# Mixture-of-experts stage: packed products over columns of one k tile, paired gate and up chunks, another merge order, an earlier count

## The chip, the cores and the metric

The kernel runs on one core of a Trainium2 chip. The metric is the device time of one execution in microseconds (us). Engines are named as in the profile: PE (TensorE matmuls), PEld (its weight loads), DVE (VectorE), ACT (ScalarE), POOL (GpSimd), SP (SyncE, which here issues the large DMAs).

## The reference, cut to what matters

Two decoder layers on 256 tokens of width 1024. The first has a dense channel mixer. The second routes each token to 2 of 8 experts; this part is what the change touches:

```python
def swiglu(x, w_gate_up, w_down):
    g, up = jnp.split(x @ w_gate_up, 2, axis=-1)
    return (jax.nn.silu(g) * up) @ w_down

def moe_swiglu(x, w_router, w_gate_up, w_down):     # w_gate_up (8, 1024, 7168), w_down (8, 3584, 1024)
    logits = (x @ w_router).astype(jnp.float32)
    top_v, top_i = lax.top_k(logits, TOP_K)
    gates = jax.nn.softmax(top_v, axis=-1)
    combine = jnp.sum(jax.nn.one_hot(top_i, N_EXPERTS, dtype=jnp.float32) * gates[..., None], axis=-2)
    y = jnp.zeros_like(x)
    for e in range(N_EXPERTS):
        y = y + combine[..., e:e + 1].astype(x.dtype) * swiglu(x, w_gate_up[e], w_down[e])
    return y
```

All is float32. The expert weights alone are 8 x 44 MB = 352 MB, each byte read once.

## The kernel before, in words

Up to 614 us the kernel does layer 0, and layer 1's token mixer and routing; none of that code changes except for line numbers. Then `moe` works through the experts, ordered by how many tokens they got: place 0 has the most, place 7 the fewest. Places 0 to 3 are the **big** ones, with 128 token slots (place 0 has a second, **far**, tile of 64 slots). Places 4 and 5 have 64 slots, 6 and 7 have 32; these are the **small** ones. `gather` collects a place's tokens into columns by a product with a one-hot matrix, and after the last product the rows are sent back with the transposed one-hot (`back`), scaled by the gate and added to `acc`.

Two generators run beside each other. `big` does places 0, 1, 2, 3 in PSUM banks `mm`; `small` does 6, 7, 4, 5 in banks `aux`. `merge` interleaves their steps by two ratios, `((42, 42), (126, 49))`: 42 steps of each, then 126 big and 49 small, with the last 8 small ones (`lead`) behind everything. A big step loads 1 MB of weights, a small step 2 MB, except the 14 small steps of the last down projection (`tail`), of 1 MB and 512 columns wide. Each load is a DMA of 512 KB into a `raw` buffer, issued by SP: from `load` (L127) for big steps, from `whole` (L157) for small ones. There are 17 `raw` buffers.

- A big step splits each raw tile into a rounded part `whi` (ACT, L181) and a remainder `wlo` (DVE, L182), and PE adds three products hi*hi, hi*lo and lo*hi, each one pass of 512 columns (the far tile holds the high and low half of its tokens side by side and needs two). A raw buffer is free after its DVE instruction.
- A small step multiplies the raw float32 weights (`plain_mm`). 64 slots use half of the array's columns, 32 a quarter, so two or four products run beside each other. Before, these are **two or four different k tiles** with the same 512 weight columns, so that each strip of PSUM holds a partial sum. `copied` (L1040) brings the rows to SBUF, and `fold` (L1049) transposes all four 128-column blocks on PE and adds the partial sums (L1052, L1057). A raw buffer is free after its last product.

Up projections go by chunks of 1024 columns, first gate, then up, and of 512 at the end (`up(c, width)`). What a step leaves for PE, such as folds and transposes, is put off by `later_on` to the next `flush`. Each engine takes its instructions in the order that the scheduler wrote.

At the end comes `overflow`: every engine loads the count `omaxi` (L1294) and branches on it (L1295); the body, for experts with more tokens than slots, is not entered in these runs. Then the last LayerNorm follows, and the store.

Of the kernel before, what the change touches and what calls it, by code (L numbers as in the profile page):

```python
# [8 lines left out]
F32 = mybir.dt.float32  # L9
# [48 lines left out]
class Body:  # L58
# [397 lines left out]
    def mixer(self, l, xT):  # L456
# [72 lines left out]
        def in_turn(products):  # L529

            made = []
            for x in products:
                self.mm(*x)
                made.append(self.made.ins)
            for x, y in zip(made, made[1:]):
                self.behind(y, x, mybir.DependencyClass.NoSync)

        def fox():
            for t in range(2):
# [3 lines left out]
                for g in range(t + 1):  # L543
# [8 lines left out]
                    in_turn((p3[b][:, i], qk["fq"][rows[b], 2 * g + i, t * 128:(t + 1) * 128],  # L552
# [12 lines left out]
                    in_turn((o[rows[b], (2 * g + i) * 128:(2 * g + i + 1) * 128],  # L565
# [7 lines left out]
        def diff():  # L573
            for t in range(2):
                o = self.o_bank()
                kw = 128 * (t + 1)
                for g, n in ([(0, 4)] if t == 0 else [(0, 2), (2, 2)]):
# [6 lines left out]
                    in_turn((p3[c][:, i], qk["dq"][c * 64:c * 64 + 64, g + i, t * 128:(t + 1) * 128],  # L584
# [341 lines left out]
    def gather(self, h, place, w, far):  # L926
# [38 lines left out]
        back = self.wk.tile([128, 256], F32R, name="back", tag="back" + "sb"[big], bufs=3 if big else 2)  # L965
# [20 lines left out]
    def plain_mm(self, outs, slots, x, k0, w, loads, first, last):  # L986


        order = []
        m = 128 // slots  # L990
        for i0 in range(0, len(w), m):
            for n, out in enumerate(outs):
                for i in range(m):
                    self.mm(out[slots * i:slots * (i + 1)], x(k0 + i0 + i), w[i0 + i][:, n * 512:(n + 1) * 512],
                            first and i0 == 0, last and i0 + m == len(w))
                    order.append(self.made.ins)
        for x in loads:
            self.behind(order[0], x.ins, mybir.DependencyClass.Sync)
        for x, y in zip(order, order[1:]):
            self.behind(y, x, mybir.DependencyClass.NoSync)  # L1000
# [16 lines left out]
    def gated(self, bks, slots, out):  # L1017

        nc = self.nc
        if slots == 128:  # L1020
            for bk in bks:
                s = self.wk.tile([128, 512], F32, name="silu", tag="silu", bufs=2)
                nc.scalar.activation(s, bk, AF.Silu)
                out.append(s)
            return
        rows = self.copied(bks)

        def f():
            for r in rows:
                x = self.pk.tile([128, 256], F32, name="gcol", tag="gcol", bufs=4)[:, :4 * slots]  # L1030
                self.fold(r, x, slots)
                nc.scalar.activation(x, x, AF.Silu)
                out.append(x)
        self.later_on(f)
# [9 lines left out]
    def fold(self, r, x, slots):  # L1044
# [5 lines left out]
        x3 = x.rearrange("p (k s) -> p k s", s=slots)  # L1050
        if slots == 32:
            nc.vector.tensor_reduce(x3, tb.rearrange("p (k a s) -> p k s a", a=4, s=32), axis=AX, op=OP.add)  # L1052
            return
# [3 lines left out]
        nc.vector.tensor_add(x3, r3, t3[:, :, 0:64])  # L1057

    def hidden(self, gs, bks, slots, cells, out, plain):

        nc = self.nc
        if slots < 128:
            rows = self.copied(bks)

            def f():
                for g, r, cell in zip(gs, rows, cells):
                    u = r[:, 256:256 + 4 * slots]
                    self.fold(r, u, slots)
                    if plain:
                        x = cell[:, :4 * slots]  # L1070
                        nc.vector.tensor_mul(x, u, g)
                        out.append(x.rearrange("p (k s) -> p k s", s=slots))
                        continue
# [17 lines left out]
    def job(self, wg, wd, tiles, gates, place, acc, banks, tail):  # L1091

# [7 lines left out]
        plain = place > 3  # L1100

        def cell(slots, pool, tag, bufs):

            if plain:
                return pool.tile([128, 256], F32, name="eh", tag=tag, bufs=bufs)
# [4 lines left out]
        def up(c, width):  # L1110

            nk = (4096 if plain else 2048) // width
            gs = [[] for _ in tiles]
            for j in range(2):
                bks = [[] for _ in tiles]
                for k0 in range(0, KT, nk):
                    src = wg(k0, nk, j * FE + c, width)
                    wpc = self.whole(src) if plain else self.piece(src)
                    for n, (slots, x, _) in enumerate(tiles):
                        if k0 == 0:  # L1120
                            bks[n] = [bank() for _ in range(width // 512)]
                        if plain:
                            self.plain_mm(bks[n], slots, x()[0], k0, *wpc, k0 == 0, k0 + nk == KT)
                        else:
                            self.tile_mm(bks[n], slots, x()[0], k0, wpc, k0 == 0, k0 + nk == KT)
                    self.flush()
                    for n, (slots, _, _) in enumerate(tiles):
                        if k0 + nk < KT:
                            continue
                        if j == 0:  # L1130
                            self.gated(bks[n], slots, gs[n])
                        else:
                            self.hidden(gs[n], bks[n], slots, [cell(slots, *tiles[n][2]) for _ in bks[n]], hid[n], plain)
                    yield 1

        def down(k0, nk, c0, width):
            last = k0 + nk == FE // 128
            src = wd(k0, nk, c0, width)
            wpc = self.whole(src) if plain else self.piece(src)
            for n, (slots, _, _) in enumerate(tiles):  # L1140
# [9 lines left out]
                if plain:  # L1150
                    self.plain_mm([dn[hf, n] for hf in hfs], slots, x, k0, *wpc, k0 == 0, last)
                else:
                    self.tile_mm([dn[hf, n] for hf in hfs], slots, x, k0, wpc, k0 == 0, last)
# [26 lines left out]
        def ups():  # L1180
            for c in range(0, FE, 1024):
                yield from up(c, min(1024, FE - c))

        def downs():
            if tail:
                steps = [(4 * i, 4, 512 * hf, 512) for hf in range(2) for i in range(7)]
            else:
                nk = 4 if plain else 2
                steps = [(nk * i, nk, 0, 1024) for i in range(28 // nk)]
            for i, (k0, nk, c0, width) in enumerate(steps):  # L1190
                down(k0, nk, c0, width)
                if k0 + nk == FE // 128:
                    end(range(c0 // 512, (c0 + width) // 512))
                yield 1
        return ups(), downs()

    def moe(self, ctx, h, routing, g, b):
# [27 lines left out]
        for place in range(1, NE):  # L1225
            if place < 4:
                tiles[place] = [lazy(place, 128, self.wk, "eh", self.neh)]
            else:
                tiles[place] = [lazy(place, 64 if place < 6 else 32, pool, "near", 8)]

        def chain(places, banks, tail=None):

            for k, place in enumerate(places):
# [4 lines left out]
                up, down = self.job(*weights(eid[place]), tiles[place], lambda: gates, place, acc, banks, place == tail)  # L1238
                yield from up
                for n, z in enumerate(down):  # L1240
                    if n == 4 and k + 1 < len(places):
                        tiles[places[k + 1]][0][1]()
# [19 lines left out]
        for x in tiles[0] + tiles[6]:  # L1262
            x[1]()
        for n, z in enumerate(merge(big, small, ((42, 42), (126, 49)), 8)):
            if n == 6:
                both, overi, mxi = next(routing)
                gates += both
            if n == 12:
# [15 lines left out]
        self.overflow(h, gates, overi, mxi, weights, eid, acc, stats)  # L1284
# [6 lines left out]
    def overflow(self, h, gates, overi, mxi, weights, eid, acc, stats):  # L1291

        nc, tc = self.nc, self.tc
        n = nc.values_load(mxi[0:1, 0:1], min_val=-S, max_val=S)  # L1294
        with tc.If(n > 0):  # L1295
# [7 lines left out]
    def rest(self, h, pos, gates, w, place, base, acc):  # L1303
# [5 lines left out]
        for t in range(2):  # L1309
            nc.vector.tensor_scalar(col[:, t:t + 1], pos[t][:, place:place + 1], -float(base), None, op0=OP.add)  # L1310
            x = self.wk.tile([128, 512], F32, name="o_hot", tag="silu", bufs=2)
# [15 lines left out]
        for c in range(7):  # L1327
# [11 lines left out]
            s = self.wk.tile([128, 512], F32, name="silu", tag="silu", bufs=2)  # L1339
# [28 lines left out]
    def run(self):  # L1368
        with ExitStack() as early, ExitStack() as later:
# [78 lines left out]
```

## Time and profile before

| | us |
|---|---|
| median of 3 runs (lowest, highest) | 1533.03 (1532.88, 1535.96) |
| the profiled execution, its own time | 1533.21 |
| its span, first to last instruction | 1531.5 |
| first expert DMA is issued | 614.3 |
| last product of the experts ends | 1513.8 |
| granted TensorE clock, mean | 0.994 |

The difference of 1.7 us between time and span lies around the execution. The page gives PE as busy for 98% of the span; but ends of matmuls are modelled there, and a PE that is busy need not be what the rest waits for. So the table's stages have to be read with the bandwidth beside them.

### The profile page before, as it was taken

What the parts mean: (1) busy time and instruction counts of PE and PEld (TensorE: products, weight loads), DVE (VectorE), ACT (ScalarE), POOL (GpSimd) and SP (SyncE); (2) the same over time, 40 slices, a digit from 0 to 9 for tenths busy, and PEclk for the clock granted to TensorE, in tenths of its full rate; (3) what the DMA queues carried; (4) which work ended last, traced back from release to release, by engine and by line L of the source; (5) the groups of instructions that cost most, each with busy time, mean ns of one, the idle gap of its engine ahead of it and who ended that gap; (6) DMA issues with size and microseconds to landing.
All of it is one profiled execution on the core that took longest, in us unless ns stands there. A gap on an engine that the chain in (4) does not pass through costs nothing. (4 is left out here: it accounts for less than half of the span.)

```text
span 1531.5 us, 24214 instructions
## 1 busy us (share of the span) xinstructions
PE 1494.3 (98%) x8782; PEld 1129.4 (74%) x8782; DVE 917.5 (60%) x1302; ACT 735.6 (48%) x1049; POOL 16.8 (1%) x43
## 2 busy tenths in 40 slices
PE   8999999999999999999999999999999999999995
PEld 6989989998798997766655665666766667666662
DVE  7556675545665666444535443766666566666774
ACT  5565444444346532354434333556564556556650
POOL 3000000000000000000000000000000000000000
PEclk9999999999999999999999999999999999999998
DMA  9644546555573330999999999999999999999992
GB/s 300 195 138 140 172 159 197 189 166 179 157 238 115 127 122 1 368 409 402 408 408 403 404 401 401 409 409 402 371 405 409 383 403 409 389 396 401 397 397 100
DMA packets 187347, 454.73 MB, mean 297 GB/s; under 512 B 13050, under 2 KB 68370, under 8 KB 187220
## 3 DMA queue, kind: packets, MB, share of 16 engines
q1 hardware_dynamic: 186432, 452.05, 79.0%
q0 software_dynamic: 784, 1.05, 0.4%
q8 instruction: 71, 1.16, 0.3%
q14 instruction: 56, 0.46, 0.1%
q10 hardware_dynamic: 4, 0.01, 0.0%
HBM read 452.00 MB, written 1.05 MB: 296 GB/s over the span
## 5 line engine op out<-in xcount | busy, mean ns | idle before, releaser
L182 DVE TENSOR_TENSOR wlo<-raw,whi 128x1024 fp32r<-128x1024 f32 (+2 forms) x524 | 617.0, 1201 | 354.7 <-ACT whi L181 349.2
L181 ACT ACTIVATE whi<-raw 128x1024 fp32r<-128x1024 f32 (+2 forms) x524 | 529.6, 1041 | 269.9 <-PE mm L92 155.8
L92 PE MATMUL mm<-hTh,wlo 128*128 128x256 f32 x672 | 192.2, 286 | 0.0
L92 PE MATMUL mm<-hTh,whi 128*128 128x256 f32 x672 | 191.4, 285 | 0.0
L92 PE MATMUL mm<-hTl,whi 128*128 128x256 f32 x672 | 190.9, 284 | 0.0
L92 PE MATMUL mm<-wlo,xh 128*128 128x512 f32 x448 | 180.0, 402 | 3.1 <-DVE wlo L182 2.6
L92 PE MATMUL mm<-whi,xl 128*128 128x512 f32 x448 | 175.3, 391 | 0.0
L92 PE MATMUL mm<-whi,eh 128*128 128x512 f32 x504 | 162.9, 398 | 0.7 <-ACT whi L181 0.7
L92 PE MATMUL aux<-raw,xs 128*32 128x512 f32 (+1 forms) x896 | 156.2, 598 | 0.0
L92 PE MATMUL mm<-whi,xh 128*128 128x512 f32 x448 | 154.7, 404 | 1.2 <-ACT whi L181 1.1
L92 PEld LDWEIGHTS mm<-hTh,wlo 128*128 128x128 f32 x672 | 128.9, 192 | 2.9 <-issue 2.0
L92 PEld LDWEIGHTS mm<-hTl,whi 128*128 128x128 f32 x672 | 128.8, 192 | 0.2
L92 PEld LDWEIGHTS mm<-hTh,whi 128*128 128x128 f32 x672 | 128.8, 192 | 0.2
L92 PEld LDWEIGHTS mm<-whi,eh 128*128 128x128 f32 x504 | 92.5, 188 | 38.3 <-issue 10.0
L92 PEld LDWEIGHTS mm<-whi,xh 128*128 128x128 f32 x448 | 80.7, 188 | 46.2 <-issue 15.7
L92 PE MATMUL mm<-wlo,eh 128*128 128x512 f32 x280 | 107.7, 398 | 0.3
L92 PEld LDWEIGHTS mm<-wlo,xh 128*128 128x128 f32 x448 | 84.1, 188 | 26.6 <-DVE wlo L182 10.2
L92 PEld LDWEIGHTS aux<-raw,xs 128*32 128x32 f32 (+1 forms) x896 | 41.4, 123 | 82.0 <-issue 77.5
L1040 ACT ACTIVATE rows<-aux 128x512 f32<-128x512 f32 x56 | 33.3, 596 | 134.5 <-PE aux L92 134.5
L92 PEld LDWEIGHTS mm<-whi,xl 128*128 128x128 f32 x448 | 84.3, 188 | 16.7 <-issue 0.8
L92 PE MATMUL aux<-raw,eh 128*32 128x512 f32 (+1 forms) x448 | 78.7, 599 | 0.0
L92 PEld LDWEIGHTS mm<-wlo,eh 128*128 128x128 f32 x280 | 52.6, 188 | 12.2 <-DVE wlo L182 0.9
(325 smaller groups left out, 1940.3 us busy)
## 6 DMA issues: line engine op xcount, KB each, us to landing
raw<-in_w_expert_gate_up SPq DMA_DIRECT2D x448, 512.0 KB, 10.1
raw<-in_w_expert_down SPq DMA_DIRECT2D x224, 512.0 KB, 9.8
raw<-in_w_in SPq DMA_DIRECT2D x36, 1024.0 KB, 5.4
raw<-in_w_ffn_gate_up SPq DMA_DIRECT2D x22, 1024.0 KB, 5.1
raw<-in_w_ffn_down SPq DMA_DIRECT2D x10, 1024.0 KB, 4.9
raw<-in_w_out SPq DMA_DIRECT2D x8, 1024.0 KB, 5.0
raw<-in_w_in SPq DMA_DIRECT2D x8, 520.0 KB, 4.9
raw<-in_w_branch_fox SPq DMA_DIRECT2D x4, 1024.0 KB, 5.0
```

The costliest lines, as they stand in the source:

```text
L92: self.made = self.nc.tensor.matmul(out, lhsT, rhs, start=start, stop=stop)
L181: return (self.nc.scalar.activation(hi, src, AF.Copy), self.nc.vector.tensor_sub(lo, src, hi.bitcast(F32)))
L182: self.nc.vector.tensor_sub(lo, src, hi.bitcast(F32)))
L1040: self.nc.scalar.activation(r, bk, AF.Copy)
```

## The change

Four things, all in the experts' stage.

1. **Columns instead of k tiles.** `plain_mm` now gives the array's halves or quarters other columns of one k tile. `cuts` says into how many column ranges a step's weights are cut: in the up projection as many as there are strips (32 slots: four ranges of 256; 64 slots: two of 512), so that each strip holds finished sums of its columns and nothing is folded. The down projection always has two cuts; in the `tail` they are 256 wide. A new `plain_job` does the small places: SiLU is read from PSUM (`gsilu`), the product with up is read from PSUM as well (`rows`, L1192), and only the hidden values are transposed (L1199). The way back is by plain float32 products of 64 rows, in pairs.
2. **Gate and up by neighbouring chunks.** Gate and up columns stand beside each other, 7 chunks of 512 each; chunks are now loaded in pairs, always 1024 columns, in the order 0, 6, 2, 8, 4, 10, 12, where chunk 6 is the last of gate and 7 the first of up. SiLU tiles live longer, so `silu` has 4 buffers, not 2.
3. **Merge** goes by `((42, 37), (126, 54))`, and place 6 is gathered ahead of place 0.
4. **The count** is loaded at the 60th merged step on all engines.

Buffers: `raw` goes from 17 to 13 of 512 KB.

```diff
-    def plain_mm(self, outs, slots, x, k0, w, loads, first, last):
-        order = []
-        m = 128 // slots
-        for i0 in range(0, len(w), m):
-            for n, out in enumerate(outs):
-                for i in range(m):
-                    self.mm(out[slots * i:slots * (i + 1)], x(k0 + i0 + i), w[i0 + i][:, n * 512:(n + 1) * 512],
-                            first and i0 == 0, last and i0 + m == len(w))
+    def plain_mm(self, out, slots, cuts, x, k0, w, loads, first, last, swap=False):
+        parts = 128 // slots
+        kk = parts // cuts
+        n = w[0].shape[1] // cuts
+        products = []
+        for i0 in range(0, len(w), kk):
+            for j in range(cuts):
+                for i in range(i0, i0 + kk):
+                    q = (j * kk + i - i0 + (parts // 2 if swap else 0)) % parts
+                    products.append((out[slots * q:slots * (q + 1), :n], x(k0 + i), w[i][:, j * n:(j + 1) * n],
+                                     first and i0 == 0, last and i0 + kk == len(w)))
+        self.in_turn(products, loads)
...
+    def plain_job(self, wg, wd, tile, gates, place, acc, banks, tail):
...
+        def hidden(b, chunks):
+            r = self.row_tile("rows")[:, :n]
+            for i, h in chunks:
+                nc.vector.tensor_mul(r[half[h]], b[half[h], :n], gate[i][half[h]])
...
+            def f():
+                tb = self.tp_bank()
+                for j in range(n // 128):
+                    cs = slice(j * 128, j * 128 + 128)
+                    nc.tensor.transpose(tb[:, cs][:, rows], r[rows, cs], self.ident[rows, rows])
...
+        def up(c):
+            b = bank()
+            for k0 in (0, 4):
+                self.plain_mm(b, slots, parts, get()[0], k0, *self.whole(wg(k0, 4, 512 * c, 1024)), k0 == 0, k0 == 4, c >= 6)
+                self.flush()
...
+        def down(k0, c0, width):
+            if k0 == 0:
+                dn[c0] = bank()
+            self.plain_mm(dn[c0], slots, 2, lambda kt: hid[kt], k0, *self.whole(wd(k0, 4, c0, width)), k0 == 0, k0 == 24)
...
+        def ups():
+            for c in (0, 6, 2, 8, 4, 10, 12):
+                yield from up(c)
...
-        for x in tiles[0] + tiles[6]:
+        for x in tiles[6] + tiles[0]:
             x[1]()
-        for n, z in enumerate(merge(big, small, ((42, 42), (126, 49)), 8)):
+        for n, z in enumerate(merge(big, small, ((42, 37), (126, 54)), 8)):
...
+            if n == 60:
+                early, (most,) = nc.values_load_multi_w_load_instructions(mxi[0:1, 0:1], min_val=-S, max_val=S)
...
-                self.weights_in(ctx, "experts_w", 17, PW // 2, 5, PW // 2)
+                self.weights_in(ctx, "experts_w", 13, PW // 2, 5, PW // 2)
```

How the order of instructions moves is seen at three places. First PE, early in the experts' stage, beside place 0's up projection (`xh`, `xl`, and `xp` for the far tile) and place 6's (`raw,xs`). Before:

```order
L92 MATMUL aux<-raw,xs 32x512 x8
L1049 MATMUL tp<-ident,rows 128x128 x4
L92 MATMUL mm<-whi,xh 128x512 x2
L92 MATMUL mm<-whi,xp 128x512 x2
L1049 MATMUL tp<-ident,rows 128x128 x4
L92 MATMUL mm<-wlo,xh 128x512
```

And now, in the same place (L1051 is the far tile's fold, which stays):

```order
L92 MATMUL aux<-raw,xs 32x256 x16
L1051 MATMUL tp<-ident,rows 128x128 x4
L92 MATMUL mm<-whi,xh 128x512 x2
L92 MATMUL mm<-whi,xp 128x512 x2
L1199 MATMUL tp<-ident,rows 128x128 x2
L92 MATMUL mm<-wlo,xh 128x512
```

A small step has 16 products of 256 columns instead of 8 of 512, and two transposes of hidden values stand where eight of a fold stood. Over the stage, transposes from `rows` go from 280 to 104.

Second SP's queue, where place 6's last up chunk was loaded (ISA sets an address up). Before:

```order
L127 DMA raw<-in_w_expert_gate_up 128x1024
L157 ISA
L157 DMA raw<-in_w_expert_gate_up 128x2x512
L157 ISA
L157 DMA raw<-in_w_expert_gate_up 128x2x512
```

And now:

```order
L127 DMA raw<-in_w_expert_gate_up 128x1024
L157 ISA
L157 DMA raw<-in_w_expert_gate_up 128x1024
L157 ISA
L157 DMA raw<-in_w_expert_gate_up 128x1024
```

Each gate and up load now has rows of 1024 columns (4 KB); the two 512-wide chunks of each place, 32 MB over the eight, had rows of 2 KB. The last down projection's 14 MB and 256 KB x 4 of LayerNorm constants keep 2 KB.

Third DVE at the end of the experts. Before:

```order
L182 TENSOR_TENSOR y<-aux,y 128x512
L1162 SCALAR_TENSOR_TENSOR acc_7068<-tp,gate_6842,acc_7068 128x512
L1162 SCALAR_TENSOR_TENSOR acc_7070<-tp,gate_6846,acc_7070 128x512
L250 BN_STATS ln_st<-acc_7068 128x6
L250 BN_STATS ln_st<-acc_7070 128x6
L1294 TENSOR_LOAD omaxi
L1295 COMPARE_AND_BRANCH
```

And now:

```order
L1238 SCALAR_TENSOR_TENSOR acc_7066<-tp,gate_6846,acc_7066 128x256
L1238 SCALAR_TENSOR_TENSOR acc_7068<-tp,gate_6850,acc_7068 128x256
L1238 SCALAR_TENSOR_TENSOR acc_7066<-mm,gate_6846,acc_7066 128x256
L1238 SCALAR_TENSOR_TENSOR acc_7068<-mm,gate_6850,acc_7068 128x256
L250 BN_STATS ln_st<-acc_7066 128x6
L250 BN_STATS ln_st<-acc_7068 128x6
L1380 COMPARE_AND_BRANCH
```

The remainder `y` and the load of the count are gone from DVE's end, and the two sums are four of half the width; the branch stays. On PE the load of the count still stands right ahead of its branch.

## Rows read from the trace of the kernel before

**Rows 1.** The page: GB/s in 40 slices of the span; DMA issues.

```profile
GB/s 300 195 138 140 172 159 197 189 166 179 157 238 115 127 122 1 368 409 402 408 408 403 404 401 401 409 409 402 371 405 409 383 403 409 389 396 401 397 397 100
...
raw<-in_w_expert_gate_up SPq DMA_DIRECT2D x448, 512.0 KB, 10.1
raw<-in_w_expert_down SPq DMA_DIRECT2D x224, 512.0 KB, 9.8
```

**Rows 2.** Busy time by stretch; the columns are named in the first row.

```profile
core 0: us, PE busy (x) PEld busy (x) DVE busy (x) ACT busy (x) POOL busy (x), PEclk, DMA share, GB/s
960.00:1040.00 80.00, 79.22 (x362) 51.92 (x361) 56.11 (x62) 46.70 (x63) 0.00 (x0) 1.00 1.03 409
1090.00:1110.00 20.00, 20.00 (x106) 15.11 (x105) 12.73 (x13) 10.04 (x14) 0.00 (x0) 1.00 0.91 338
1190.00:1210.00 20.00, 20.00 (x92) 12.19 (x90) 11.87 (x11) 12.48 (x15) 0.00 (x0) 1.00 0.95 361
1300.00:1360.00 60.00, 60.00 (x270) 38.79 (x271) 41.30 (x43) 35.13 (x46) 0.00 (x0) 1.00 1.01 389
1480.00:1490.00 10.00, 10.00 (x44) 6.94 (x43) 7.35 (x6) 6.08 (x7) 0.00 (x0) 1.00 1.05 387
1500.00:1501.00 1.00, 1.00 (x7) 0.19 (x4) 0.63 (x1) 0.00 (x0) 0.00 (x0) 1.00 0.43 164
1501.00:1513.40 12.40, 12.40 (x56) 4.48 (x56) 4.01 (x6) 0.00 (x0) 0.00 (x0) 1.00 0.01 5
```

**Rows 3.** Waits of SP's DMA queue, 614.3 to 957 us: total, times, longest.

```profile
SPq L157 <- DMA raw<-in_w_expert_gate_up: 74.2, 102, 1.9
```

**Rows 4.** The same waits, 957 to 1500 us.

```profile
SPq L127 <- PE aux L92: 109.3, 69, 6.6
...
SPq L127 <- DVE wlo L182: 34.7, 42, 2.6
```

**Rows 5.** PE's groups by shape, 614.3 to 1514 us (count, busy us, mean ns).

```profile
L92 PE MATMUL aux<-raw,xs 128*64 128x512 f32 x448 | 102.3, 598 | 0.0
L92 PE MATMUL aux<-raw,xs 128*32 128x512 f32 x448 | 53.9, 598 | 0.0
...
L1049 PE MATMUL tp<-ident,rows 128*128 128x128 f32 x280 | 41.6, 276 | 1.5 <-ACT rows L1040 1.5
```

**Rows 6.** Timeline of one 32-slot step, 708 to 711 us (start, duration).

```profile
708.76 1.92 PE L92 MATMUL aux<-raw,xs 128*32 128x512 f32 x16
709.22 0.13 PEld L92 LDWEIGHTS aux<-raw,xs 128*32 128x32 f32 x4 [0.30 <-issue]
...
710.62 0.74 PE L92 MATMUL mm<-whi,xh 128*128 128x512 f32 x2
```

**Rows 7.** Timeline of layer 0's attention at 103 us, products on two halves of the array.

```profile
103.06 1.09 PE L92 MATMUL o<-pT,fv 128*64 128x128 f32 x16
```

**Rows 8.** Timeline of the end, 1495 to 1521 us.

```profile
1497.88 1.19 PE L92 MATMUL tp<-y,back 128*128 128x512 f32 x4
...
1504.99 8.80 PE L92 MATMUL aux<-raw,eh 128*64 128x512 f32 x40
...
1513.84 0.60 ACT L181 ACTIVATE y<-aux 128x512 fp32r<-128x512 f32 x1 [15.25 <-PE aux L92]
...
1515.75 1.41 DVE L1162 SCALAR_TENSOR_TENSOR acc<-tp,gate,acc 128x512 f32<-128x512 f32 x2 [0.59 <-PE tp L92]
1517.08 1.27 DVE L250 BATCH_NORM_STATS2 ln_st<-acc 128x6 f32<-128x512 f32 x2
1520.93 0.28 DVE L256 BATCH_NORM_AGGREGATE ln_mv<-ln_st 128x2 f32<-128x12 f32 x2 [2.58 <-DVEq L1295]
```

**Rows 9.** Line L1294 on DVE's and PE's queues, and L1295 (durations min/median/max in ns, first and last start).

```profile
L1294 DVEq TENSOR_LOAD <-omaxi x1: 545/545/545, 1517.2 to 1517.2; - x1
...
L1295 PEldq COMPARE_BRANCH  x1: 3875/3875/3875, 1515.8 to 1515.8; - x1
L1295 DVEq COMPARE_BRANCH  x1: 72/72/72, 1517.8 to 1517.8; - x1
```

More of the change, by code (lines that the diff above doesn't have):

```diff
@@ L984, in tile_mm, with in_turn @@
                         self.mm(out, act, part[:, n * 512:(n + 1) * 512], a and j == 0, z and j == len(steps) - 1)
[L986 to L999 removed]
+    def plain_mm(self, out, slots, cuts, x, k0, w, loads, first, last, swap=False):
[10 more added lines that the diff above has]
+        self.in_turn(products, loads)
+    def in_turn(self, products, after=()):
+        made = []
+        for x in products:
+            self.mm(*x)
+            made.append(self.made.ins)
+        for x in after:
+            self.behind(made[0], x.ins, mybir.DependencyClass.Sync)
+        for x, y in zip(made, made[1:]):
             self.behind(y, x, mybir.DependencyClass.NoSync)
@@ L1029, in f @@
             for r in rows:
[L1030 to L1031 removed]
+                x = self.pk.tile([128, 256], F32, name="gcol", tag="gcol", bufs=5)
+                self.fold(r, x)
                 nc.scalar.activation(x, x, AF.Silu)
@@ L1042, in copied, with fold @@
         return out
-    def fold(self, r, x, slots):
+    def fold(self, r, x):
         nc = self.nc
@@ L1056, in fold, with hidden @@
         nc.scalar.activation(r3, t3[:, :, 64:128], AF.Copy)
-        nc.vector.tensor_add(x3, r3, t3[:, :, 0:64])
-    def hidden(self, gs, bks, slots, cells, out, plain):
+        nc.vector.tensor_add(x.rearrange("p (k s) -> p k s", s=64), r3, t3[:, :, 0:64])
+    def hidden(self, gs, bks, slots, cells, out):
         nc = self.nc
@@ L1066, in f @@
                 for g, r, cell in zip(gs, rows, cells):
[L1067 to L1073, printed above, removed]
+                    u = r[:, 256:512]
+                    self.fold(r, u)
                     nc.vector.tensor_mul(u, u, g)
@@ L1108, in cell @@
             return pool.tile([128, 512], F32R, name="eh", tag=tag, bufs=bufs)
[L1110 to L1123, printed above, removed]
-                        else:
[L1125 to L1134, printed above, removed]
+        gs = [[[] for _ in range(7)] for _ in tiles]
+        def up(c):
+            nk = 2
+            bks = [[] for _ in tiles]
+            for k0 in range(0, KT, nk):
+                src = wg(k0, nk, 512 * c, 1024)
+                wpc = self.piece(src)
+                for n, (slots, x, _) in enumerate(tiles):
+                    if k0 == 0:
+                        bks[n] = [bank() for _ in range(2)]
+                    self.tile_mm(bks[n], slots, x()[0], k0, wpc, k0 == 0, k0 + nk == KT)
+                self.flush()
+                for n, (slots, _, _) in enumerate(tiles):
+                    for i in range(c, c + 2) if k0 + nk == KT else ():
+                        bk = [bks[n][i - c]]
+                        if i < 7:
+                            self.gated(bk, slots, gs[n][i])
+                        else:
+                            self.hidden(gs[n][i - 7], bk, slots, [cell(slots, *tiles[n][2])], hid[n])
+                yield 1
         def down(k0, nk, c0, width):
@@ L1138, in down @@
             src = wd(k0, nk, c0, width)
-            wpc = self.whole(src) if plain else self.piece(src)
+            wpc = self.piece(src)
             for n, (slots, _, _) in enumerate(tiles):
@@ L1149, in down @@
                         dn[hf, n] = bank()
[L1150 to L1153, printed above, removed]
+                self.tile_mm([dn[hf, n] for hf in hfs], slots, x, k0, wpc, k0 == 0, last)
             self.flush()
@@ L1180, in ups @@
         def ups():
-            for c in range(0, FE, 1024):
-                yield from up(c, min(1024, FE - c))
+            for c in (0, 6, 2, 8, 4, 10, 12):
+                yield from up(c)
         def downs():
[L1185 to L1193, printed above, removed]
-                yield 1
+            for k0 in range(0, 28, 2):
+                down(k0, 2, 0, 1024)
+                if k0 == 26:
+                    end(range(2))
+                yield 1
@@ L1228, in moe @@
             else:
-                tiles[place] = [lazy(place, 64 if place < 6 else 32, pool, "near", 8)]
+                tiles[place] = [lazy(place, 64 if place < 6 else 32, pool, "near", 5)]
         def chain(places, banks, tail=None):
@@ L1241, in chain @@
                     if n == 4 and k + 1 < len(places):
-                        tiles[places[k + 1]][0][1]()
+                        for x in tiles[places[k + 1]]:
+                            x[1]()
                     yield z
@@ L1267, in moe @@
                 gates += both
+            if n == 60:
+                early, (most,) = nc.values_load_multi_w_load_instructions(mxi[0:1, 0:1], min_val=-S, max_val=S)
+                order = ctx.enter_context(ExitStack())
+                for x in early:
+                    if x.ins.engine in (mybir.EngineType.DVE, mybir.EngineType.Activation):
+                        order.enter_context(tc.issue_after(x.ins))
+            if n == 62:
+                order.close()
             if n == 12:
@@ L1283, in moe @@
         stats(1)
-        self.overflow(h, gates, overi, mxi, weights, eid, acc, stats)
+        self.overflow(h, gates, overi, most, weights, eid, acc, stats)
         for t in range(2):
```

104 lines of the change are left out of this document (78 added, 26 removed).

## The prediction

> **What bounds the kernel now.** I read the page's bandwidth row first: from the 17th slice on, about 614 us, it stands near 400 GB/s to the end [rows 1]. The experts' stage moves 672 loads of 512 KB, 352 MB, and 1 MB of constants; no edit changes these bytes. So the first question is what rate the DMA could hold, the second why it holds less, the third what comes after the last byte.
>
> The best long stretch holds 409 GB/s [rows 2]. At 1480 to 1490 us, where only the last down projection's 512-wide loads run, it is 387 though the DMA engines are just as busy (share 1.05): rows of 2 KB cost 5.5% [rows 2]. At 1090, 1190 and 1300 us the rate falls to 338, 361 and 389, and there PE is busy for the whole of the stretch [rows 2]. The waits of SP say why: up to 957 us SP mostly waits for an earlier DMA, so the DMA itself sets the pace [rows 3]; after that it waits 109 us for PE to finish small products and 35 us for DVE's splits, that is, for `raw` buffers to come free [rows 4]. PE lags behind the data by nearly all 17 buffers.
>
> The end shows the lag directly. The weights are in at about 1500.5 us (the DMA is 0.43 busy in the microsecond from 1500, then 0.01) [rows 2], but PE works on until 1504.99 + 8.80 = 1513.8 us without a gap [rows 8]. These 13.3 us are backlog. So two bounds lie on each other: DMA with some 2% lost, and PE, which is nearly full and comes 13 us late.
>
> **The change part by part.**
>
> *Wider rows.* 32 MB of gate and up loads go from 2 KB rows to 4 KB rows. 33.6 MB take 86.7 us at 387 GB/s and 82.0 us at 409: **-4.7 us** of DMA time. Nothing hides it, since the DMA is never idle in the stage.
>
> *Fewer transposes.* The fold group is 280 instructions with 41.6 us of PE, 0.149 us each [rows 5]. 176 of them go: **-26 us** of PE work in the 899 us from the first load to the last product. The copies and reduces of the folds leave ACT and DVE, which are not what PE waits for at the end; I count nothing for them.
>
> *Products on other columns.* A 32-slot up step is 32 records of 256 columns instead of 16 of 512. One step now takes 708.76 to 710.62, 1.86 us [rows 6], four records in parallel, so about 0.43 us for each four. I cost the new step at the same 1.86 us. From below: twice as many products cannot take less, the columns being the same. From above: no gain from halving columns gives 3.44 us for the products. The nearest row is layer 0's attention: sixteen records of 128 columns on two halves of the array span 1.09 us, last drain included [rows 7]. Eight pairs in at most that is 0.136 us a pair for a quarter of the columns that now take 0.43 us; so the time follows the columns even at a quarter of the width. 64-slot steps keep 512 columns but for the last projection.
>
> The Trainium skill, "TensorE: Matmul & The Clock Gate", section "Part 3: Packing small matmuls — row/col tiling", says that a weight load runs beside products in flight only if it goes to other rows of the array. All strips here use all 128 rows, so by the page each group of four would wait for its weight loads. The trace disagrees: the second set of loads ends long before the products that it stands beside (0.13 us of loads, then 0.30 us idle, in each 0.43 us) [rows 6].
>
> *Merge.* Five 2 MB steps of 32 slots, 9.3 us of PE, go from beside place 0 to beside places 1 to 3. They bring 10 MB for which the DMA needs 25.6 us at 409 GB/s, so in the stretch where PE is late the work per byte falls; beside place 0 it rises, in a stretch where SP waited for the DMA. No separate gain: it lets the relief by the transposes reach both stretches.
>
> *13 buffers.* The DMA needs some loads in flight: with 10.1 us from issue to landing and 1.28 us for each at 409 GB/s, eight are queued at once on the median [rows 1]. Fewer do as well: the dips show what too few cost, 389 GB/s over 60 us [rows 2]. With 13, PE can be at most about ten loads, 13 us, late before the DMA starves. I take no cost, because PE will be less late; the bound is below.
>
> *Starved stretches.* Against 409 the three dips cost 20 x (1 - 338/409) = 3.5, 20 x (1 - 361/409) = 2.3 and 60 x (1 - 389/409) = 2.9 us, together 8.7 [rows 2]. With 26 us of PE work gone PE needs 873 us for what the DMA brings in no less than 866 (339 MB at 409 GB/s, 14.7 at 387). It stops being late for long: **-8.7 us**. Bound: 0.
>
> *The backlog.* The last 8 small steps take PE 8.80/5 = 1.76 us each [rows 8] and the DMA 2.7 us at 387 GB/s, so PE gains 7.5 us on the data, less three returns of 1.19 us [rows 8]: 4 us. If PE is 8 us late when they start, about what 13 buffers and a DMA that sets the pace leave, it ends 4 us after the last byte instead of 13.3: **-9.3 us**. Bounds: one last step and its wait, 2.2 us, and 13.3.
>
> *The end.* After PE, ACT copies 0.60 us and DVE makes a remainder before the last products; then two sums of 0.70, two statistics, the count and the branch [rows 8]. The remainder goes (0.7 us, of which the return products in plain float32 may take half back: the trace has two records for each of them, as for the `raw` products), and DVE's load of the count, 0.55 us [rows 9]. The branch's wait of 2.58 us stays [rows 8]: its target is the same, and it follows each engine's branch, not the load. PE still loads the count late, and its branch lasts to 1519.7, ahead of DVE [rows 9]. **-1.0 us**; bounds 0 and -1.3.
>
> Sum: 4.7 + 8.7 + 9.3 + 1.0 = 23.7 us from the profiled execution's 1533.2: 1509.5, say **1510 us**. That execution is 0.2 us above the median of the runs shown, so the same number stands for both.
>
> **The rivals.**
>
> *The lag stays.* The late splits may lie in the written order of ACT and PE, not in load. For it: a PE that never pauses over 60 us [rows 2] looks the same whether it has too much work or starts its work late. Against: after 957 the buffers are what SP waits for. Then the 9.3 us do not come: 1519; with half of the starved time as well, 1524.
>
> *13 buffers starve the DMA.* If more than about ten buffers are held on average, the rate is that of the dips throughout. 353 MB at 389 GB/s instead of 409 cost 44 us, against 23.7 won: 1554. Half of the stage in that state gives 1532, which is the point from which it decides. For it: SP waited for buffers even with 17 [rows 4]. Against: those waits follow PE's load, which falls.
>
> *Quarter products do not follow their columns.* If four of 256 columns take the 0.43 us of four of 512, 28 up steps take 1.72 us more, 48 us in a stretch without room: 1558. If only the weight loads come into the open, 8 groups x 0.13 us x 28 steps are 29 us of PE [rows 6], which eats the 26 us of transposes: 1531, no change. That is the time by the page's rule named above. [rows 7] speak against both.
>
> *All of it comes.* The DMA at its floor (614.3 + 866 + 2.5 us to the first landing = 1482.8, 17.7 less than now), 2.2 us of lag and 1.3 at the end are 30.1 us: 1503.
>
> **How the numbers follow.** The forecast as summed, 1503 to 1518, has 0.60. The lag that stays, 1518 to 1528, 0.20. All of it and more, below 1503, 0.06. Starving buffers 0.09, of which 0.07 slower. Quarter products 0.05: 0.03 slower, 0.02 no change (the page's rule among these, 0.02). 0.2%, 3 us, is about what a measurement of this kernel tells from no change. Faster: 0.60 + 0.20 + 0.06 = 0.86; same: 0.02 + 0.02 = 0.04; slower: 0.10. The range is 1503 to 1528: it leaves out 0.06 below and 0.14 above. It holds both cases that share the sign; the slower ones lie outside.
>
> **What would show it.** Right: 408 GB/s or more in the stretches that hold gate and up loads, without dips below 390; SP's waits for `PE aux` far under 109 us; the last load in at 1485 to 1489; PE's last product 2 to 7 us behind it; four 256-column products in about 0.22 us; DVE's gap ahead of the last LayerNorm still about 2.6 us. Wrong: a rate below 400 with SP waiting for buffers (the 13), or a 32-slot step over 2.5 us (the quarters), or 10 us and more from the last byte to PE's end (the order).

## The result and the profile after

The changed kernel takes 1524.22 us (median of 6 runs, 1523.02 to 1528.02), the kernel before 1533.81 on the same chip: a ratio of 0.9939, 95% interval 0.9925 to 0.9954. It is faster by 9.4 us by the ratio (9.6 between the medians), inside the range and far from the 23.7 us of the sum. The profiled execution took 1526.24 us, 2.0 above the median, and has a span of 1524.4 us (before 1531.5); that is why spans further down differ by 7.1 us only.

The windows of the changed kernel come first; they answer to [rows 2].

```profile
core 0: us, PE busy (x) PEld busy (x) DVE busy (x) ACT busy (x) POOL busy (x), PEclk, DMA share, GB/s
618.00:628.00 10.00, 9.79 (x46) 9.50 (x46) 3.98 (x10) 4.40 (x7) 0.00 (x0) 0.50 1.02 408
...
640.00:660.00 20.00, 20.00 (x139) 13.35 (x141) 6.57 (x6) 8.88 (x12) 0.00 (x0) 1.00 0.96 350
770.00:790.00 20.00, 19.24 (x121) 13.85 (x120) 7.90 (x8) 10.01 (x16) 0.00 (x0) 1.00 0.95 353
1250.00:1310.00 60.00, 60.00 (x278) 38.67 (x275) 37.89 (x39) 29.91 (x35) 0.00 (x0) 1.00 0.99 380
960.00:1040.00 80.00, 74.65 (x347) 47.10 (x346) 49.68 (x47) 43.13 (x48) 0.00 (x0) 1.00 1.03 409
1090.00:1110.00 20.00, 20.00 (x90) 14.38 (x91) 12.13 (x11) 8.80 (x9) 0.00 (x0) 1.00 1.03 410
...
1300.00:1360.00 60.00, 59.30 (x261) 37.13 (x260) 35.80 (x36) 29.30 (x34) 0.00 (x0) 1.00 1.02 404
...
1500.00:1503.20 3.20, 3.20 (x32) 2.15 (x30) 0.99 (x2) 0.00 (x0) 0.00 (x0) 1.00 0.72 267
1503.20:1505.20 2.00, 2.00 (x22) 1.29 (x19) 0.00 (x0) 0.00 (x0) 0.00 (x0) 1.00 0.06 20
1505.20:1507.70 2.50, 2.35 (x20) 1.26 (x16) 0.00 (x0) 0.00 (x0) 0.00 (x0) 1.00 0.00 0
```

The reader sees three things. The dips of before are gone (1090: 410 GB/s, 1300: 404), but new ones stand at 640, 770 and 1250 us. From 618 to 628 us TensorE had half of its clock, 1.2 GHz. And the DMA ends in two steps: most of it by about 1503, then 2 us at 20 GB/s and a share of 0.06, which is one of 16 engines. Looked at as closely, the kernel before does the same, which the long last window of [rows 2] had hidden:

```profile
1500.00:1501.00 1.00, 1.00 (x7) 0.19 (x4) 0.63 (x1) 0.00 (x0) 0.00 (x0) 1.00 0.43 164
1501.00:1504.00 3.00, 3.00 (x13) 1.16 (x14) 1.41 (x2) 0.00 (x0) 0.00 (x0) 1.00 0.06 19
1504.00:1506.00 2.00, 2.00 (x10) 0.98 (x12) 1.37 (x3) 0.00 (x0) 0.00 (x0) 1.00 0.00 0
```

So the last byte of before landed at 1503.9 us, not 1500.5, and TensorE ended 9.9 us behind it, not 13.3.

The timeline of TensorE at the start of the stage, in the changed kernel, shows place 6's gather (32 slots) and then place 0's (128 slots), both slow, and the first products with weights at 629.26 (place 6) and 630.68 (place 0):

```profile
616.91 5.81 PE L92 MATMUL tp<-hot,h 128*128 128x32 f32 x30 [0.22 <-DVE hot L925]
...
623.20 6.14 PE L92 MATMUL tp<-hot,h 128*128 128x128 f32 x32 [0.21 <-ACT xs L946]
629.26 1.48 PE L92 MATMUL aux<-raw,xs 128*32 128x256 f32 x18
630.68 0.50 PE L92 MATMUL mm<-whi,xh 128*128 128x512 f32 x1
```

In the kernel before, place 0's products with weights were at work ten microseconds earlier:

```profile
620.30 0.71 PE L92 MATMUL mm<-whi,xh 128*128 128x512 f32 x2
```

PE's groups by shape over the stage (to [rows 5]): the transposes from `rows` have 8.4 + 6.0 + 1.6 = 16.0 us instead of 41.6, and quarters of 256 columns 55.6 us instead of 53.9.

```profile
L92 PE MATMUL aux<-raw,xs 128*32 128x256 f32 x896 | 55.6, 382 | 0.0
...
L1051 PE MATMUL tp<-ident,rows 128*128 128x128 f32 x56 | 8.4, 280 | 1.5 <-ACT rows L1042 1.5
L1199 PE MATMUL tp<-ident,rows 128*128 128x128 f32 x36 | 6.0, 276 | 0.0
L1199 PE MATMUL tp<-ident,rows 64*128 64x64 f32 x12 | 1.6, 239 | 0.0
```

One 32-slot step in the timeline (to [rows 6], there 1.92 us for the same 2 MB), the weight loads beside it:

```profile
700.96 1.45 PEld L92 LDWEIGHTS aux<-raw,xs 128*32 128x32 f32 x32 [0.35 <-issue]
700.97 1.93 PE L92 MATMUL aux<-raw,xs 128*32 128x256 f32 x32
```

The end (to [rows 8]): `y` is copied at 1507.72, DVE's gap is 2.12 us.

```profile
1498.47 9.21 PE L92 MATMUL aux<-raw,eh 128*64 128x256 f32 x80
...
1507.72 0.38 ACT L1235 ACTIVATE y<-aux 128x256 f32<-128x256 f32 x1 [15.83 <-PE aux L92]
...
1513.86 0.28 DVE L256 BATCH_NORM_AGGREGATE ln_mv<-ln_st 128x2 f32<-128x12 f32 x2 [2.12 <-DVEq L1380]
```

The account, in us; the last column is the first experiment, explained below:

| | forecast | before | changed | place 0 gathered first |
|---|---|---|---|---|
| first load issued | | 614.3 | 614.05 | 614.5 |
| last byte, after the first load | -13.4 | 889.6 | 891.1 (+1.5) | 882.6 (-7.0) |
| TensorE's last product behind it | -9.3 | 9.9 | 2.6 (-7.3) | 2.6 (-7.3) |
| from there to the span's end | -1.0 | 17.7 | 16.7 (-1.0) | 16.8 (-0.9) |
| span | -23.7 | 1531.5 | 1524.4 (-7.1) | 1516.4 (-15.1) |

Each column is one profiled execution, so a difference of 2 us between columns says little by itself.

### The profile page after: what moved, and what is told of

Same layout as the page of the kernel before. It is cut to its first block, busy times and chain, and to the rows that moved or that the text cites. A ratio compares the mean times of both kernels' runs of the same rounds, so it can differ in the third digit from the quotient of the medians.

```text
span 1524.4 us, 24838 instructions
## 1 busy us (share of the span) xinstructions
PE 1482.7 (97%) x9174; PEld 1138.1 (75%) x9174; DVE 897.4 (59%) x1242; ACT 715.7 (47%) x966; POOL 16.9 (1%) x43
## 5 line engine op out<-in xcount | busy, mean ns | idle before, releaser
L92 PE MATMUL aux<-raw,xs 128*32 128x256 f32 (+1 forms) x1344 | 157.9, 454 | 2.1 <-issue 1.6
L92 PE MATMUL mm<-whi,xh 128*128 128x512 f32 x448 | 150.5, 404 | 0.9 <-ACT whi L181 0.9
L92 PEld LDWEIGHTS aux<-raw,xs 128*32 128x32 f32 (+1 forms) x1344 | 56.4, 118 | 83.7 <-issue 61.1
L92 PE MATMUL aux<-raw,eh 128*32 128x512 f32 (+2 forms) x560 | 79.1, 512 | 2.1 <-DMA raw<-in_w_expert_down 1.8
L92 PEld LDWEIGHTS aux<-raw,eh 128*64 128x64 f32 (+1 forms) x560 | 28.8, 125 | 38.8 <-issue 30.1
```

What stands on the lines that cost most here:

```text
L92: self.made = self.nc.tensor.matmul(out, lhsT, rhs, start=start, stop=stop)
```

## The experiments

Each ratio is to the kernel before on the same chip. "Last byte" counts from the first load, read from the DMA packets of the profiled execution.

| run | ratio, 95% interval | last byte | PE behind it |
|---|---|---|---|
| changed kernel | 0.9939 (0.9925 to 0.9954) | 891.1 | 2.6 |
| e1 place 0 gathered first | 0.9893 (0.9878 to 0.9909) | 882.6 | 2.6 |
| e2 14 buffers | 0.9920 (0.9906 to 0.9933) | 885.3 | 2.6 |
| e3 11 buffers | 0.9995 (0.9986 to 1.0004) | 899.9 | 2.6 |
| e4 before, 13 buffers | 1.0001 (0.9992 to 1.0010) | 894.4 | 5.9 |
| e5 e1 + old merge | 0.9915 (0.9901 to 0.9928) | 882.4 | 3.4 |
| e6 e1 + 14 buffers | 0.9906 (0.9893 to 0.9920) | 884.2 | 2.6 |
| e7 e1 + 15 buffers, 4 split parts | 0.9902 (0.9887 to 0.9917) | 884.0 | 2.6 |
| e8 e1 + 192 transposes | 0.9985 (0.9976 to 0.9994) | 894.5 | 7.0 |
| e9 before, place 6 first | 1.0024 (1.0015 to 1.0034) | 894.9 | 9.6 |
| e10 e1, 12.7 us of PE left out | 0.9899 (0.9884 to 0.9915) | 884.6 | 2.6 |
| e11 e1, 25.4 us of PE left out | 0.9887 (0.9871 to 0.9902) | 883.6 | 2.6 |
| e12 e7 + merge between | 0.9906 (0.9892 to 0.9920) | 882.0 | 5.0 |
| e13 e11 + 1344 instructions | 0.9883 (0.9868 to 0.9898) | 882.2 | 2.6 |
| e14 e11 + 336 longer instructions | 0.9906 (0.9891 to 0.9921) | 885.6 | 2.6 |
| e15 e1, loads of 1 MB | 1.0049 (1.0036 to 1.0063) | 899.0 | 9.0 |
| e16 e1, 152 us of PE left out | 0.9896 (0.9880 to 0.9913) | 885.0 | 2.6 |
| e17 e11 + 15 buffers, 4 split parts | 0.9887 (0.9870 to 0.9903) | 881.6 | 2.6 |

**First theories.** "Too few buffers": 13 starve the DMA. "Late start": the gather order and the clock behind it cost 9 us that TensorE cannot make up. "Merge order": the new ratios load the wrong stretch.

```diff
-        for x in tiles[6] + tiles[0]:
+        for x in tiles[0] + tiles[6]:
```

> The changed kernel (1524.2) with place 0 gathered ahead of place 6 again, all else as changed. Theory 'late start': TensorE has work without a pause from its first expert product to its last, so the 9 to 10 us by which that first product came late (630.7 us, before 620.3, with half of the granted clock for 10.2 us in between) reach the end: 1514 to 1517, the granted clock 1.00 at 616 to 630 us. Theory 'too few buffers': the start costs only the dips at 640 to 700 us (370, 331, 379 and 389 GB/s, together 4 us), and the later dips stay: 1520 to 1523. Theory 'merge order': 1522 to 1524.

Measured: 0.9893, 7.0 us less than the changed kernel's ratio gives (0.0046 x 1534). TensorE's timeline has the gather back in 4.17 us and products with weights at 620.52, and its windows the clock at 1.00 and 409 GB/s where the changed kernel had 350:

```profile
616.59 4.17 PE L92 MATMUL tp<-hot,h 128*128 128x128 f32 x32 [0.91 <-DVE hot L928]
620.52 0.71 PE L92 MATMUL mm<-whi,xh 128*128 128x512 f32 x2
```

```profile
618.00:628.00 10.00, 10.00 (x79) 9.28 (x79) 5.51 (x13) 5.19 (x8) 0.00 (x0) 1.00 1.02 409
...
640.00:660.00 20.00, 20.00 (x163) 14.15 (x156) 5.80 (x7) 8.81 (x16) 0.00 (x0) 1.00 1.02 409
...
1250.00:1310.00 60.00, 60.00 (x279) 38.01 (x278) 35.86 (x34) 30.60 (x34) 0.00 (x0) 1.00 0.99 382
...
1494.00:1497.00 3.00, 3.00 (x30) 2.01 (x28) 0.00 (x0) 0.00 (x0) 0.00 (x0) 1.00 0.17 62
1497.00:1500.00 3.00, 2.39 (x22) 1.26 (x16) 0.00 (x0) 0.33 (x1) 0.00 (x0) 1.00 0.00 0
```

0.9893 x 1533.8 is 1517.4, at the edge of what "late start" gave. The later dips stay.

Buffers: the second argument of `weights_in` is the edit.

```diff
-                self.weights_in(ctx, "experts_w", 13, PW // 2, 5, PW // 2)
+                self.weights_in(ctx, "experts_w", 14, PW // 2, 5, PW // 2)
```

> The changed kernel with 14 raw buffers instead of 13 (the room is taken from the row tiles, 5 instead of 6). Theory 'too few buffers': one more load of 1.28 us in hand in each of some seven spells in which the DMA starves, so 3 to 8 us less: 1516 to 1521. Theory 'late start': TensorE's work sets the end, and a load more in hand changes nothing: 1523 to 1525.

> The changed kernel with 11 raw buffers instead of 13. Theory 'too few buffers': the DMA runs empty in every stretch, 10 to 25 us more: 1534 to 1550. Theory 'late start': with TensorE the bound two loads less in hand cost at most 2.6 us in two or three places: 1524 to 1530.

> The kernel before with 13 raw buffers instead of 17, all else as before. It prices the four buffers where TensorE is late for most of the stage. Theory 'too few buffers': 8 us more or above, 1541 to 1555, with rates like those of the dips (338 to 389 GB/s) over long stretches. Theory 'late start': TensorE is the bound already, so the buffers cost little: 1533 to 1538.

Measured: 14 take away some 3 us (the intervals of e2 and the changed kernel overlap), 11 add 8.6 us. In the kernel before (e4) 13 cost nothing, though they are short: the last byte comes 4.8 us later, and SP waited 125.5 us for PE at L157 alone after 957 us, but TensorE's backlog set the end anyway.

```profile
SPq L157 <- PE aux L92: 125.5, 39, 7.5
```

> The kernel before with one edit: place 6 gathered ahead of place 0. Theory 'late start': the first expert product comes 8 to 11 us later here too, TensorE has no slack to make it up, and 17 buffers don't help: 1.004 to 1.007 of the time before. Theory 'too few buffers' (the late start costs only where 13 buffers run empty): 1.000 to 1.002.

Measured: 1.0024, 3.7 us, between the two. The first product with split weights came at 629.96 us, the clock was 0.66 from 618 to 628. The late start costs without the rest of the change, but in the kernel before, with 17 buffers and a backlog that is there anyway, over half of the 10 us doesn't show; which of the two hides it was not tried.

**With place 0 first, what holds the rest?**

> Place 0 gathered first (the first experiment: 0.989 of the time before), and also the merge ratios of before, (42, 42) and (126, 49). Theory 'merge order': the new ratios took five light 2 MB steps away from the first stretch and made the second stretch too heavy in small steps; with the old ones the dips at 1190 to 1330 us (360 to 394 GB/s) shrink and 3 to 6 us go: 0.985 to 0.987. Theory 'TensorE still late': the second stretch loses five steps that are light for TensorE per byte, so its dips grow, while the first stretch has more: 0.990 to 0.995. Theory 'too few buffers': no change, 0.988 to 0.990.

> Place 0 gathered first and 14 raw buffers (row tiles 5 instead of 6). Theory 'too few buffers': the dips that are left (770 to 790, 830 to 850, 1250 to 1290 us) lose some 1 us each, 0.985 to 0.987. Theory 'TensorE still late': TensorE works without a pause from one of these dips to the next, and a load more in hand is used up once and not won again: 0.988 to 0.990.

> Place 0 gathered first, 15 raw buffers, the room taken from the split weights (4 of whi and wlo instead of 5). Theory 'too few buffers': 2 to 6 us less, 0.985 to 0.988. Theory 'TensorE still late': 0.988 to 0.992, with TensorE waiting a little more for splits.

> Place 0 gathered first, 15 raw buffers (4 of whi and wlo), merge ratios (42, 40) and (126, 51), between the old and the new ones: a try for the best version. TensorE was idle for some 12 us of the stage with either ratio, at other places. Theory 'TensorE still late': the work is the same, so 0.987 to 0.990. Theory 'merge order': 0.983 to 0.987.

Measured: none differs from e1 beyond the intervals, 0.9902 to 0.9915. With place 0 first, "merge order" falls, and so does "too few buffers" from 13 up, but for effects under some 3 us, which these intervals would not show. "TensorE still late" fitted all four, so it was put to the test from both sides: transposes added (`list(range(n // 128)) * 5` in `hidden`), then products left out (the third product of `tile_mm`):

```diff
-                        steps = [(h, wh), (h, wl), (x[1](k0 + i, 0), wh)]
+                        steps = [(h, wh), (h, wl), (x[1](k0 + i, 0), wh)][:2 if k0 + i >= skip else 3]
```

> Place 0 gathered first, and each transpose of the small places' hidden values made five times into the same place: 192 more transposes on TensorE, about what the fold's 176 were. It prices the work that the change took away. Theory 'TensorE still late': TensorE's work reaches the end nearly in full, 192 x 0.11 to 0.149 us = 21 to 29 us more: 1.003 to 1.008. Theory 'too few buffers': the DMA sets the end, and half or less of it shows: 0.992 to 0.997.

> Place 0 gathered first, and in the up projections of places 0 to 3 the product of the low part of the tokens with the last of the eight k tiles is left out: 56 products of 512 columns, 0.227 us each, 12.7 us of TensorE less, which with what the change gave makes up the 26 us that were forecast. Theory 'TensorE still late': 7 to 12 us less, 0.981 to 0.985. Theory 'the DMA sets the end' (dips have another cause than TensorE): 0.988 to 0.990.

> As the one before, with the last two k tiles left out: 112 products, 25.4 us of TensorE less. Theory 'TensorE still late': now the DMA has its 409 GB/s nearly throughout, the last byte lands at 1483 to 1488 us, and the time falls by less than twice the step before: 0.975 to 0.980. Theory 'the DMA sets the end': 0.987 to 0.990.

Measured: more work costs, some 14 us (0.9985 against 0.9893) for 192 transposes that keep TensorE busy for 18.7 us, and TensorE ends 7.0 us behind the last byte. Less work gains nothing: 0.9899 and 0.9887. "TensorE still late" falls. e1 stands where more work of TensorE can be felt and less can not: something else ends there.

**What ends there.** In all runs of the changed kernel that gather place 0 first, but for e8 and e15, the last byte lands 881.6 to 885.6 us after the first load, and at the end the rate is that of one engine for some microseconds (of two in e13, below). By the packets' times 8 KB loads of the queue that the profile calls "instruction" lie in that engine's chain: in e17, below, one of 0.33 us at 1493.81, while it moves data alone. So the next runs changed the number of instructions:

```diff
+                    for j in range(4):
+                        self.nc.vector.tensor_copy(scr[0:1, j:j + 1], lo[0:1, j:j + 1].bitcast(F32))
```

> The kernel of the run with two k tiles left out (0.9887), and behind each of the 336 splits four copies of a single element on VectorE: 1344 more instructions with nearly no data. Theory 'instruction loads on one DMA engine': 1344 x 64 bytes are some 10 more loads of 8 KB on the late engine, 0.32 us each and 0.43 us of slow packets behind it, 7 to 8 us later for the last byte: 0.992 to 0.995. Theory 'the DMA engine is late for another reason': the copies take idle time of VectorE, 0.988 to 0.990.

> The same, with one copy of 256 elements on 128 partitions behind each split in place of the four: as much or more time of VectorE, a quarter of the instructions. Theory 'instruction loads on one DMA engine': 2 to 3 more loads of 8 KB, 1.5 to 2 us: 0.989 to 0.991. If the four copies cost by VectorE's time, this one costs as much as they: 0.992 to 0.995.

> Place 0 gathered first; loads of 1 MB into 7 raw buffers (row tiles 5 instead of 6) in place of 512 KB into 13: SP has half of its instructions, some 1340 fewer, and the DMA half of the loads. Theory 'instruction loads on one DMA engine': 10 fewer loads of 8 KB, the last byte 7 us earlier, if the coarser buffers don't starve the DMA: 0.984 to 0.987; with starving 0.988 to 0.995, but then the last byte of a DMA that was never short would still come sooner. Theory 'another reason': 0.989 or more.

Measured: the queue that loads them has 48 packets in the stage of e13 (the row below, 614 to 1500 us) and 37 in that of e11, and e13 is no slower (0.9883); e14, at 0.9906, is not clearly slower than e11 either. So 11 more of these loads don't cost 7 to 8 us. But that doesn't clear them, for the added ones went elsewhere: at the end of e13 two engines move data alone, 54 GB/s at a share of 0.15 (second row), where e17 has one (below). The added instructions of VectorE made a second engine about as late as the first, and the last byte did not move (882.2 against 883.6).

```profile
q14 instruction: 48, 0.39, 0.1%
...
1492.00:1496.60 4.60, 3.54 (x32) 2.19 (x28) 0.00 (x0) 0.00 (x0) 0.00 (x0) 1.00 0.15 54
```

e15 has 23 such loads, against 37 in e1, and no late engine at its end, as "instruction loads" would have it. It is still no test: 7 large buffers made SP wait 243.6 us for PE at L127, and it lost 24 us to e1.

Last, TensorE was taken out of the question: e16 leaves out 152 us of its work, e17 gives e11 two buffers more.

> Place 0 gathered first, and in places 0 to 3 every product of the low part of the tokens or hidden values with the weights' high part is left out (672 products of 0.227 us, 152 us of TensorE less; the loads are the same). Theory 'TensorE in bursts': TensorE is late only around changes of place and chunk, with so little work never; the dips go, and the last byte lands 868 to 874 us after the first load: 0.979 to 0.983 of the time before. Theory 'the DMA itself': the last byte still lands 880 to 885 us after the first load: 0.987 to 0.990.

> The kernel of the run with two k tiles left out (0.9887, last byte 883.6 us after the first load), with 15 raw buffers, the room taken from the split weights (4 instead of 5). Theory 'TensorE in bursts': two loads more in hand take up half of what the dips cost, 2 to 4 us: 0.986 to 0.988. Theory 'the DMA itself': 0.988 to 0.990.

Measured: no gain, 0.9896 and 0.9887. e17's windows show that the dips are gone, 406 GB/s at 1250 to 1310 us where e1 had 382, and that it brings nothing: 383 GB/s up to 1488, then from 1490 on for over 5 us one engine's share, 0.07.

```profile
640.00:660.00 20.00, 20.00 (x161) 13.63 (x159) 5.70 (x7) 7.98 (x14) 0.00 (x0) 1.00 1.03 409
...
1250.00:1310.00 60.00, 60.00 (x285) 39.47 (x284) 36.91 (x35) 32.27 (x37) 0.00 (x0) 1.00 1.02 406
1486.00:1488.00 2.00, 2.00 (x20) 1.18 (x18) 1.88 (x5) 0.00 (x0) 0.00 (x0) 1.00 1.04 383
1490.00:1494.00 4.00, 2.53 (x23) 1.67 (x23) 0.00 (x0) 0.00 (x0) 0.00 (x0) 1.00 0.07 26
1494.00:1496.30 2.30, 1.49 (x14) 0.86 (x10) 0.00 (x0) 0.00 (x0) 0.00 (x0) 1.00 0.06 19
1496.30:1498.00 1.70, 1.12 (x11) 0.94 (x13) 0.00 (x0) 0.00 (x0) 0.00 (x0) 1.00 0.00 0
```

Its SP waits after 957 us are nearly all for earlier DMAs:

```profile
SPq L127 <- DMA raw<-in_w_expert_gate_up: 116.6, 157, 1.5
SPq L157 <- DMA raw<-in_w_expert_gate_up: 80.4, 108, 1.5
SPq L127 <- DMA raw<-in_w_expert_down: 56.8, 75, 1.5
SPq L157 <- DMA raw<-in_w_expert_down: 45.0, 62, 1.5
SPq L127 <- PE mm L92: 6.5, 24, 0.4
```

"The DMA itself" stands.

The trace of e17 also says where the late engine loses its time. It keeps, for each load, the 16 landing times of the 16 engines' parts; their last against their eighth is how late the late engine is. From 930 to 1495 us there are 24 instruction loads of 8 KB. At 16 of them, most some 41 us apart, the last landing falls back by 0.58 to 0.74 us each; at the other 8 it doesn't, and between them it doesn't either. From 930 to 1470 us the landings lose 8.4 us against 409 GB/s, and the 13 steps in between add up to 8.7 (e16: 8.1, and 12 steps of 8.2). That the others must wait shows in SP's queue: of the 402 loads issued from 960 to 1484 us, 396 were issued within 0.2 us (median 0.12) after the last landing of the load eight before. So the late engine, one that also brings in a series of instruction loads, sets the pace of the stage from there on. This is read from traces; no run took those loads away from it.

## Why the prediction was wrong

**What was right.** The quarter products follow their columns (1.93 us a step) and the weight loads stay hidden. By the page's rule in "TensorE: Matmul & The Clock Gate", Part 3, of the Trainium skill the step would have grown by an estimated 8 x 0.13 us [rows 6]; it grew by 0.01. The transposes fell by 25.6 us (said: 26). 4 KB rows run at 404 to 410 GB/s outside the dips. The end gained the 1.0 us forecast, though in part by another way: DVE's wait ahead of the last LayerNorm, which was to stay at 2.58 us, fell to 2.12.

**The backlog: right mechanism, start mis-sized.** PE is now 2.6 us behind the last byte, one last step of 1.95 us and 0.6 us before it, near the lower bound of 2.2. But it had been 9.9 us late, not 13.3, so the gain was 7.3, not 9.3 us: the last window of [rows 2] was 12.4 us long, and its 5 GB/s were 3 us of one engine. The lag left is below the 4 us of the sum, and the lag of before was below its 13.3; the two errors partly cancel.

**The step that failed: "wider rows" and "starved stretches", the 13.4 us of DMA time.** Both were counted against 409 GB/s, with a floor of 866 us for the bytes and the last byte at 1482.8 at best, 868.5 us after the first load. No kernel came under 881.6, 13 us above that floor, not even with 152 us of TensorE's work gone, or without dips. So of the 889.6 us of before no run won more than 8.0, whatever the dips and rows cost; removing dips does not shorten a DMA whose last engine is late. What the floor left out is the instruction loads on that engine: the 16 steps counted in e17 are 10.7 of the 13 us. The rival "all of it comes" rested on the same floor.

**What was never costed: place 6 gathered first.** The sum called the merge free and passed over the gather. It made the first product with split weights 10 us late, half the clock included, against 13 buffers that hold 13 x 1.28 = 16.6 us. The buffers filled, the DMA ran short (350 GB/s at 640 to 660), and the last byte came 8.5 us later than in e1 (891.1 against 882.6). That is the sign of being wrong that the prediction named for the 13 buffers, a rate below 400 with SP waiting for buffers. SP's largest wait in the changed kernel from 614.05 to 957 us (total, times, longest):

```profile
SPq L157 <- PE aux L92: 75.6, 63, 6.1
```

So "13 buffers" at no cost failed here too: not by TensorE's load, as the rival had it, but by its start. How much 17 would have hidden in the changed kernel was not measured; one more (e2) took away some 3 us, and e3 shows that 11 would have cost another 8.6 us.

With that order undone the sum is 7.0 + 7.3 + 0.9 = 15.2 us, and e1 is the best full version found: 0.9893 against 0.9939. That the changed kernel's 1524 us is also what the prediction gave for "the lag stays; with half of the starved time as well" is chance: the lag went, to 2.6 us.

**What stays open.** Whether the stage gets shorter when the late engine's instruction loads are fewer or lie on several engines: the traces point to them, e13 added loads to another engine, and no run took any away alone. Why the lag builds up only from about 860 us in e17, though such loads come all through the stage, is open too. The Trainium skill, "DMA: Bandwidth & Descriptors", section "Latency and other measured facts", lists two engines (7 and 15) that are usually slower in traces, and guesses at rings of software DMAs. An engine that ends late agrees, a slower one doesn't: alone it moves 26 GB/s, which is a full sixteenth of 409. And the guess does not fit a stage in which the loads are issued by SP and no software queue moves a packet. Which engine it is, the trace doesn't tell. Which of the dips left in e1 belong to which change of place was not tried either.

## What to carry to other kernels

Before taking a transfer floor from the best rate, look at the last microseconds in windows narrow enough to reach zero: a share of 1/16 there is one late engine, and it, not the mean rate, ends the stage. Relieving an engine that trails the DMA wins its lag and no more; ask what the DMA can do with that engine out of the way. And in an edit of order at the start of a stage, read the first product's time and the granted clock: what is lost there no later stretch gives back where the DMA has no slack.

## What the runs showed of the hardware that was not expected

- The granted clock was 0.50 (1.2 GHz) from 618 to 628 us in the changed kernel, where place 6's products of 32 columns stood at the head of the stage and place 0's of 128 columns behind them (0.66 over the same stretch in e9); with 32 products of 128 columns at the head it stayed at 1.00, also through place 6's own products from 627.3 to 631 us (e1). The pause of TensorE ahead was the same, 0.9 us. Why is not shown.
- In 16 of the 19 kernels one DMA engine of 16 landed its part of the last load 1.4 to 6.1 us after the next-to-last engine, latest where TensorE held least back (6.1 us in e16 and e17). In e13 the last two engines, 0.4 us apart, came 3.8 us behind the other fourteen. In e8 and e15, where TensorE held the DMA back, it was 0.5 us and less.
- An instruction load of 8 KB on the late engine made that engine's landings 0.58 to 0.74 us later (e17), and most loads after 960 us were issued 0.12 us after the last landing of the one eight before, so one engine's delay became the stage's.
- Adding 1344 VectorE instructions to e11 cost nothing measurable (0.9883 against 0.9887), though it made a second DMA engine late.
